# One decoder block on one core: other places in the input stage, quarter rows for the last block, and w_down's sums at every fourth product

## The chip, the cores and the metric

The kernel runs on one core of a Trainium2 chip. The metric is the device time of one execution in microseconds. A core has five engines that run their own instruction streams side by side: TensorE (PE, matmuls, with its weight loads as PEld), VectorE (DVE), ScalarE (ACT), GpSimd (POOL) and SyncE (SP), which here does nothing but issue transfers. Transfers can also be issued by ACT and POOL; all of them run on the same 16 DMA engines. An instruction waits for what it needs at its place in its engine's stream, and everything behind it on that engine waits too.

## The reference

One layer: RMSNorm, one wide input projection, two mixers side by side (a gated causal mixer over chunks of 128 positions, and a dilated window attention), a gated merge, an output projection with residual, then a gated MLP with a causal convolution, and a final RMSNorm. Sequence 1024, width 1024, MLP width 2816, everything in float32.

```python
h = rms_norm(x, mix_norm_g)
proj = h @ w_in                       # 1024 x 5888, split into z_a | q | k | v | gates
y_a = chunked_spatial_gating(gelu(z_a), gmlp_norm_g, w_spatial, b_spatial)
q, k = rope(q, positions), rope(k, positions)
y_b = dilated_mixture_attention(q, k, v)
merged = sigmoid(g_A) * (y_a @ w_branch_a) + sigmoid(g_B) * (y_b @ w_branch_b)
x = x + merged @ w_out
h2 = rms_norm(x, ffn_norm_g)
a, val = split(h2 @ w_up)
x = x + (gelu(causal_dwconv3(a)) * val) @ w_down
return rms_norm(x, final_norm_g)
```

## The kernel before

**Arithmetic.** Every float32 product is made of three fast ones: an operand is split into a high part, copied by ACT into the fast format ("hi"), and a low part, the difference, made by DVE or POOL ("lo"); hi·hi, hi·lo and lo·hi are added up in PSUM. On top of that the large products are done with a Strassen-like scheme of seven half-size products per pair of column blocks, named P1 to P7 and run in the order P1, P6, P2, P7, P5, P4, P3. In the input stage one such product is 12 matmuls of 128x512 (`in_product`, line 541). P2 is added into the PSUM bank of P1, P4 into that of P7, P3 into that of P5, so P4 can only begin when DVE has read P7's result out of its bank (line 576), and P3 only when it has read P5's (line 578). The bank's owner and its follower are two places apart, so DVE has the length of one product for that.

**Stages.** (1) `beginning`: the first two column blocks are computed plainly from the raw, not yet normalised x (tile `pl`, line 614), while x arrives in eight slices per half, `x_half(kt, h)`; the rows' root mean squares come from x in row layout (`square_row`, `root`), are put on a diagonal (`diagonal`, line 418), spread over the partitions by TensorE (`spread`, line 424), and multiplied into x (`scale_x`, line 484). `raw_left(h, kt)` makes hi (line 478, ACT) and lo (line 479, DVE) of the raw x; `left_of` makes those of the scaled x and of its sums (lines 448, 449, 454, 455). The first half is needed with the opposite sign, which its diagonal carries. A chain of small DVE steps for the rotary tables (`rot_tables`, run by `some(n)`) is strewn in between. (2) The remaining column blocks through `in_product`, with attention beside them. (3) From the last attention block on, DVE also makes sums of w_down's quarters for the last stage: `wd_load(kt)` loads four tiles of 256 KB (line 1057), `wd_sums(kt)` makes four sums of them (line 1068, 128x512 each) and stores them (tile `wT`, line 1070), for kt from 0 to 10, with two sets of buffers. (4) Branch products, w_out, the MLP's products (lines 1403 to 1932). (5) The down projection (tile `dn`, line 2195) into four blocks of rows for each half; its last product P3 is closed block by block, and a block is finished by an addition (line 2263), a sum of squares (line 2220), `finish_rms` (lines 2316 and 2321), and two halves of a row that are scaled and stored: the lower by ACT on ACT's queue (lines 2228, 2229), the upper by DVE on SP's queue (lines 2230, 2233).

**What sets the order.** TensorE's instructions stand in the order in which the code is written, over the whole kernel. Those of DVE and ACT do so in `beginning`, in the first 18 products after it, and at the end of the kernel; elsewhere a scheduler places them, and it places SP's transfers everywhere, by estimated costs.

## Time and profile before

| | us |
|---|---|
| median of 3 runs | 1364.97 |
| lowest and highest of them | 1363.93, 1366.61 |
| the profiled execution's own time | 1365.51 |
| its span from first to last instruction | 1363.6 |
| PE, DVE, ACT, POOL busy in the span | 1353.7, 1034.4, 645.0, 307.3 |

The span leaves out 1.9 us of the execution's time, and the profiled execution stands 0.54 us above the median. In a timeline a row gives the start, the time that the merged instructions take, the engine, the line, the operation, output and input tiles, the sizes, a count, and in brackets how long the engine had been idle and what ended that. Matmuls follow each other faster than one takes, so the start of one row to the start of the next is the measure, not the sum of durations.

### The profile page before, as it was taken

Reading aid. Unit: us, or ns where it says so; the run is one execution under the profiler, and the core shown is the slowest. Engines: PE = TensorE matmul, PEld = TensorE weight load, DVE = VectorE, ACT = ScalarE, POOL = GpSimd, SP = SyncE. Lnnn points to the kernel's source line nnn. Section 1 sums busy time; section 2 is a strip of 40 time slices with the busy share of each in tenths; the row PEclk is TensorE's granted clock in tenths of the full one; section 3 lists DMA queues with packets and bytes.
Section 4 is the critical chain, followed back from the end, with each engine's and each line's share of the span. In section 5 each row is a group of like instructions: output and inputs, shape, how many; then the busy total and the mean of one; then the engine's idle time right before and its main releaser. Section 6 shows DMA issues by size and latency. Waiting matters only on the chain.

```text
span 1363.6 us, 19146 instructions
## 1 busy us (share of the span) xinstructions
PE 1353.7 (99%) x6408; PEld 1126.2 (83%) x6408; DVE 1034.4 (76%) x1878; ACT 645.0 (47%) x1267; POOL 307.3 (23%) x301
## 2 busy tenths in 40 slices
PE   9999999999999999999999999999999999999997
PEld 8878888888888888888888888888888888888886
DVE  6988686767877987759789878676666668676674
ACT  7762555556543325435456344433343335354453
POOL 1123000001330000210011236666555653000002
PEclk9999999999999999999999999999999999999999
DMA  9535553544438994884751133333323327986663
GB/s 339 118 97 178 132 171 102 156 151 129 134 111 278 324 322 171 285 276 150 252 151 59 62 101 108 117 102 121 118 102 105 108 101 278 387 308 218 203 203 123
DMA packets 144577, 236.99 MB, mean 174 GB/s; under 512 B 13920, under 2 KB 57952, under 8 KB 144480
## 3 DMA queue, kind: packets, MB, share of 16 engines
q1 hardware_dynamic: 141952, 231.53, 51.5%
q0 software_dynamic: 1088, 2.10, 0.9%
q10 hardware_dynamic: 1440, 2.16, 0.4%
q8 instruction: 50, 0.82, 0.2%
q14 instruction: 47, 0.39, 0.1%
HBM read 167.77 MB, written 64.29 MB: 170 GB/s over the span
## 4 chain that ended last, share of the span: by engine, by line
PE 95%; DVE 1%; DMA 1%; ACT 1%; SPq 1%; issue 0%; POOL 0%; ACTq 0%; DVEq 0%; POOLq 0%
PE in_P L541 25%; PE uP L1932 21%; PE dn L2195 15%; PE up L1932 8%; PE wo_P L1764 6%; PE pa L1403 5%; PE pl L614 3%; PE pu L917 2%; PE pu L1912 2%; PE pb L1403 2%; PE pp L901 1%; PE sc L862 1%; PE sc L863 1%; SPq L757 1%; PE ht L1668 1%; PE pm L734 0%
## 5 line engine op out<-in xcount | busy, mean ns | idle before, releaser
L541 PE MATMUL in_P<-R,G 128*128 128x512 f32 x1008 | 243.9, 394 | 0.0
L541 PEld LDWEIGHTS in_P<-R,G 128*128 128x128 f32 x1008 | 185.5, 188 | 37.7 <-issue 0.3
L2195 PE MATMUL dn<-R 128*128 128x512 f32 x924 | 209.6, 389 | 0.0
L2195 PEld LDWEIGHTS dn<-R 128*128 128x128 f32 x924 | 173.4, 188 | 36.0
L170 ACT ACTIVATE R<-up 128x512 fp32r<-128x512 f32 x130 | 78.5, 626 | 119.3 <-DVE up L279 45.3
L312 ACT ACTIVATE G<-wr 128x512 fp32r<-128x512 f32 x126 | 78.9, 628 | 101.2 <-PE in_P L541 60.9
L541 PE MATMUL in_P<-G,G 128*128 128x512 f32 x504 | 123.5, 394 | 0.6 <-DVE C L576 0.3
L1932 PE MATMUL uP<-G,R 128*128 128x512 f32 x504 | 121.2, 389 | 0.0
L1932 PE MATMUL uP<-R 128*128 128x512 f32 x504 | 121.1, 389 | 0.0
L1932 PE MATMUL up<-G,R 128*128 128x512 f32 x504 | 120.5, 389 | 0.0
L1932 PEld LDWEIGHTS up<-G,R 128*128 128x128 f32 x504 | 94.6, 188 | 20.2
L1932 PEld LDWEIGHTS uP<-G,R 128*128 128x128 f32 x504 | 94.6, 188 | 19.8
L1932 PEld LDWEIGHTS uP<-R 128*128 128x128 f32 x504 | 94.6, 188 | 19.7
L541 PEld LDWEIGHTS in_P<-G,G 128*128 128x128 f32 x504 | 92.5, 188 | 20.6 <-issue 1.1
L313 DVE TENSOR_TENSOR G<-wr,G 128x512 fp32r<-128x512 f32 x126 | 88.2, 700 | 26.0 <-ACT G L312 24.8
L171 POOL TENSOR_TENSOR R<-up,R 128x512 fp32r<-128x512 f32 x55 | 82.7, 1506 | 58.8 <-ACT R L170 53.7
L171 DVE TENSOR_TENSOR R<-up,R 128x512 fp32r<-128x512 f32 x75 | 67.1, 898 | 18.4 <-ACT R L170 18.2
L170 ACT ACTIVATE R<-db 128x512 fp32r<-128x512 f32 x77 | 48.1, 626 | 57.6 <-PE dn L2195 46.6
L171 DVE TENSOR_TENSOR R<-db,R 128x512 fp32r<-128x512 f32 x77 | 53.6, 699 | 26.3 <-ACT R L170 26.1
L1403 PE MATMUL pa<-R,G 128*128 128x512 f32 x288 | 67.9, 389 | 0.0
L968 POOL TENSOR_TENSOR ld<-ld,w 128x256 f32<-128x256 f32 x16 | 11.3, 725 | 233.5 <-DVE w L956 233.5
L1403 PEld LDWEIGHTS pa<-R,G 128*128 128x128 f32 x288 | 54.0, 188 | 11.2
(286 smaller groups left out, 2438.4 us busy)
## 6 DMA issues: line engine op xcount, KB each, us to landing
up<-in_w_up_dram SPq DMA_DIRECT2D x44, 512.0 KB, 3.6
wr<-in_w_in_dram SPq DMA_DIRECT2D x42, 512.0 KB, 4.1
dA<-gd SPq DMA_DIRECT2D x55, 256.0 KB, 4.8
wd<-in_w_down_dram SPq DMA_DIRECT2D x44, 256.0 KB, 5.1
wT<-wd SPq DMA_DIRECT2D x44, 256.0 KB, 3.8
dS<-gS SPq DMA_DIRECT2D x44, 256.0 KB, 4.4
db<-wT SPq DMA_DIRECT2D x44, 256.0 KB, 4.4
gd<-Y SPq DMA_DIRECT2D x42, 256.0 KB, 2.0
```

The source lines that it names most:

```text
L170: nc.scalar.activation(hi, src, AF.Copy)
L171: fn = lambda: lo_eng.tensor_tensor(lo, src, f32(hi), ALU.subtract)
L312: lambda: nc.scalar.activation(op[:, 0], src, AF.Copy),
L313: lambda: nc.vector.tensor_tensor(op[:, 1], src, f32(op[:, 0]), ALU.subtract),
L541: nc.tensor.matmul(acc, op[:, w, kt, :], left[LEFT[name], kt][:, a, :], start=opened and i == 0, stop=i == len(HIGH_FIRST) - 1, skip_group ...
L614: nc.tensor.matmul(lead_banks[b][:, cs], raw_x[h, kt][:, a, c * P : (c + 1) * P], lead_op(kt, w, cs), start=kt == 0 and p == 0 and cs.star ...
L917: nc.tensor.matmul(pu[:, h * HD : (h + 1) * HD], self.pT[:, i, :], vt[:, h * HD : (h + 1) * HD], start=i % n == 0, stop=i % n == n - 1,)
L1403: nc.tensor.matmul(acc, unit[a][kt // 4][:, kt % 4, :], two(R, 8 * h + kt)[:, b, :], start=n == 0 and i == 0, stop=n == len(kts) - 1 and i ...
L1764: nc.tensor.matmul(acc, left[LEFT[name], kt][:, a, blk * P : (blk + 1) * P], out_ops[s][:, w, :], start=name not in SHARED and kt == 0 and ...
L1912: nc.tensor.matmul(acc, plain_up[which, k][:, w, kt, :], left[f"A{h + 1}{k + 1}", kt][:, a, :], start=n == 0 and i == 0, stop=n == KT - 1 ...
L1932: nc.tensor.matmul(acc, op[:, w, kt, :], left[LEFT[name], kt][:, a, :], start=opened and i == 0, stop=i == len(HIGH_FIRST) - 1, skip_group ...
L2195: nc.tensor.matmul(accs[blk], dops[s][:, 0, a, blk * P : (blk + 1) * P], dops[s][:, 1, w, :], start=SEQ[j] not in CONTINUES and kt == 0 an ...
```

## The change

The change has four groups of edits.

*Input stage.* The load of `positions` goes from ACT's queue (a step of the rotary chain) to SP's queue, ahead of x's fourth slice. The diagonals are made by ACT instead of DVE, both with a positive sign; the first half's minus goes into `ngain`, a copy of the norm's gains that POOL negates once, which `scale_x` then reads. Six rotary steps instead of three of them stand before the second wave of splits, so the chain runs three steps ahead from there. The spread of the first half stands after the first four matmuls of kt 6 instead of before them. The low part of the second half's first slices is written after the squares, and the second pair of slices before the rotary steps. In the first product's place, ACT reads out P1's bank before it makes P6's high part.

*w_down's sums.* They are taken up at every fourth product, counted from the product before the stage, instead of at each P1 and P5.

*Residual.* Two blocks are loaded by one transfer.

*Last block.* `last_blocks` takes the place of the last call: the block before it is scaled and stored first, its lower half on SP's queue; the last block's upper half is added, squared, scaled and stored in two quarters, with one more addend in `finish_rms`.

```diff
+    pos = lent[:, 11 * NB * (ROT // 2) :][:, 0:NB].bitcast(I32)
     for kt in range(1, KT):
+        if kt == 3:
+            nc.sync.dma_start(pos, positions)
         if kt == 6:
             load_rows(0, range(4))
...
-            nc.vector.tensor_scalar(dg, ident, rs, (-1.0, 1.0)[h], ALU.mult, ALU.mult)
+            nc.scalar.activation(dg, ident, AF.Copy, scale=rs)
...
+    ngain = lent[:, 6 * P - KT : 6 * P]
     def scale_x(h, kt, bc):
-        xs = x_half(kt, h)
-        nc.vector.scalar_tensor_tensor(xs, xs, chan[:, kt : kt + 1], bc, ALU.mult, ALU.mult)
+        xs, gain = x_half(kt, h), (ngain, chan)[h]
+        nc.vector.scalar_tensor_tensor(xs, xs, gain[:, kt : kt + 1], bc, ALU.mult, ALU.mult)
...
         both(lead_parts(5))
-        some(6)
+        some(9)
...
+        nc.gpsimd.tensor_scalar(ngain, chan[:, 0:KT], -1.0, None, ALU.mult)
         root(0)
-        both(raw_left(0, 6, 1))
+        both(raw_left(0, 6, 1), lead_parts(6))
         diagonal(0)
-        both(lead_parts(6))
         both(raw_left(0, 7, 1), lead_parts(7))
-        bc0 = spread(0)
-        lead_step(first, 6)
-        both(raw_left(1, 0))
+        for p in range(3):
+            if p == 1:
+                bc0 = spread(0)
+            for b in first:
+                lead_pass(b, 6, p)
+        h1_hi, h1_lo = raw_left(1, 0)
+        h1_hi()
...
         root(1)
+        h1_lo()
         for kt in range(KT):
             scale_x(0, kt, bc0)
+        both(raw_left(1, 2))
+        some(3)
         diagonal(1)
-        some(3)
-        both(raw_left(1, 2), raw_left(1, 4), raw_left(1, 6))
+        both(raw_left(1, 4), raw_left(1, 6))
...
-        p6[0]()
         x_sum(2, 1)
         in_product(FIRST, "P1")
+        p6[0]()
         p6[1]()
...
-        if wd is not None and name in ("P1", "P5"):
-            wd_sums(wd_step - 1)
-            wd_load(wd_step)
+        if wd is not None:
+            if wd_step % 4 == 0:
+                wd_sums(wd_step // 4 - 1)
+                wd_load(wd_step // 4)
             wd_step += 1
...
+    def store_lower(b, rs, queue):
+        nc.scalar.activation(Y[:, b, lower], Y[:, b, lower], AF.Copy, scale=rs)
+        queue.dma_start(out_t[:, b, lower], Y[:, b, lower])
+    def store_upper(b, rs, cs):
+        nc.vector.scalar_tensor_tensor(
+            Y[:, b, cs], Y[:, b, cs], rs, final_bc[:, cs], ALU.mult, ALU.mult
+        )
+        nc.sync.dma_start(out_t[:, b, cs], Y[:, b, cs])
+    def last_blocks(acc):
+        b = 3
+        ahead = finish_rms(nc, small, mhalf, sqs[b - 1], f"f_{b - 1}", nc.vector)
+        store_lower(b - 1, ahead, nc.sync)
+        quarter = [slice(HALF + i * 256, HALF + (i + 1) * 256) for i in range(2)]
+        for i, cs in enumerate(quarter):
+            nc.vector.tensor_tensor(
+                Y[:, b, cs], Y[:, b, cs], acc[:, i * 256 : (i + 1) * 256], ALU.add
+            )
+            jk = dp.tile([P, HALF], F32, name=f"fj_{b}_{1 + i}", tag="fj")
+            nc.scalar.activation(
+                jk[:, 0:256], Y[:, b, cs], AF.Square, accum_out=sqs[b][:, 1 + i : 2 + i]
+            )
+        store_upper(b - 1, ahead, quarter[0])
+        rs = finish_rms(nc, small, mhalf, sqs[b], f"f_{b}", nc.gpsimd, nc.vector)
+        store_upper(b - 1, ahead, quarter[1])
+        store_lower(b, rs, nc.scalar)
+        for cs in quarter:
+            store_upper(b, rs, cs)
```

Three places in the instruction streams follow; line numbers of the changed kernel are its own.

ACT in the input stage, second half of x, before the change: `C` with `ms_x` are the squares of rows, `pl` the plain product's result, `G<-X` and `R<-X` the high parts of x.

```order
L400 ACTIVATE C_105,ms_x_368<-C_105 128x1024
L631 ACTIVATE C_103<-pl_188,rs_x_320 128x512
L478 ACTIVATE G_76<-X 128x2x512
L478 ACTIVATE G_77<-X 128x2x512 x2
L448 ACTIVATE R<-X 128x2x512 x2
L631 ACTIVATE C_103<-pl_190,rs_x_320 128x512
```

The same place on ACT with the change:

```order
L403 ACTIVATE C_105,ms_x_371<-C_105 128x1024
L636 ACTIVATE C_103<-pl_189,rs_x_324 128x512
L481 ACTIVATE G_76<-X 128x2x512
L421 ACTIVATE YC<-ident,rs_x_379 128x128 x4
L481 ACTIVATE G_77<-X 128x2x512 x2
L451 ACTIVATE R<-X 128x2x512 x2
L636 ACTIVATE C_103<-pl_191,rs_x_324 128x512
```

Four instructions that write the second diagonal (`YC<-ident`) now stand on ACT between the first pair of high parts and the next two; another four stand ahead of x's last slice of the first half.

SP's transfers at the start of the w_down stage, before: `wd_0` and `wd_1` are the loads for kt 0 and 1, `wT` the stores of the sums.

```order
L666 DMA gated<-C_103 128x512
L1057 DMA wd_0_4280<-in_w_down_dram 128x512
L1057 DMA wd_0_4282<-in_w_down_dram 128x512
L1057 DMA wd_0_4284<-in_w_down_dram 128x512
L1057 DMA wd_0_4286<-in_w_down_dram 128x512
L1057 DMA wd_1_4363<-in_w_down_dram 128x512
L1057 DMA wd_1_4365<-in_w_down_dram 128x512
L1057 DMA wd_1_4367<-in_w_down_dram 128x512
L1057 DMA wd_1_4369<-in_w_down_dram 128x512
L1070 DMA wT_157<-wd_0_4286 128x512
L1070 DMA wT_155<-wd_0_4282 128x512
```

The same with the change:

```order
L1062 DMA wd_0_4267<-in_w_down_dram 128x512
L671 DMA gated<-C_103 128x512
L1328 DMA ya<-mixd 128x1024 x2
L1075 DMA wT_158<-wd_0_4267 128x512
L1075 DMA wT_156<-wd_0_4263 128x512
L1075 DMA wT_157<-wd_0_4261 128x512
L1075 DMA wT_159<-wd_0_4265 128x512
L1062 DMA wd_1_4346<-in_w_down_dram 128x512
L1062 DMA wd_1_4348<-in_w_down_dram 128x512
L1062 DMA wd_1_4350<-in_w_down_dram 128x512
L1062 DMA wd_1_4352<-in_w_down_dram 128x512
```

The loads for kt 0 now stand ahead of the last `gated` store and of two loads of `ya`, and those for kt 1 behind the four stores of the sums of kt 0, which wait for DVE.

ACT at the end of the kernel, before: `fj` is a square of a half row of a block, `Y<-Y,fr_f` the scaling of its lower half.

```order
L2220 ACTIVATE fj_1_11626,fsq_10661<-Y 128x512
L2228 ACTIVATE Y<-Y,fr_f_11611 128x512
L2229 DMA out_dram<-Y 128x512
L2220 ACTIVATE fj_1_11650,fsq_10666<-Y 128x512
L2228 ACTIVATE Y<-Y,fr_f_11635 128x512
L2229 DMA out_dram<-Y 128x512
L2228 ACTIVATE Y<-Y,fr_f_11659 128x512
L2229 DMA out_dram<-Y 128x512
```

And with the change:

```order
L2232 ACTIVATE fj_1_11623,fsq_10658<-Y 128x512
L2246 ACTIVATE Y<-Y,fr_f_11608 128x512
L2247 DMA out_dram<-Y 128x512
L2246 ACTIVATE Y<-Y,fr_f_11644 128x512
L2267 ACTIVATE fj_1_11649,fsq_10663<-Y 128x256
L2267 ACTIVATE fj_2_11652,fsq_10663<-Y 128x256
L2246 ACTIVATE Y<-Y,fr_f_11660 128x512
L2247 DMA out_dram<-Y 128x512
```

The scaling of the third block (`fr_f_11635`, now `fr_f_11644`) has moved ahead of the last block's squares, which are two of half the width, and its store has left ACT's stream.

39 lines of the change are left out of this document (18 added, 21 removed).

## The prediction

> **What bounds the kernel now.** I read the page's first part, then the chain that ended last, then TensorE's own timeline where it isn't gapless, and last the rows of the other engines there.
>
> ```profile
> PE 1353.7 (99%) x6408; PEld 1126.2 (83%) x6408; DVE 1034.4 (76%) x1878; ACT 645.0 (47%) x1267; POOL 307.3 (23%) x301
> ...
> 1147.06 209.45 PE dn L2195 x924
> ```
>
> TensorE is busy for 99% of the span, and no matmul is added or taken away. In the down projection 924 matmuls take 209.45 us without a wait, 0.2267 us each; that is my measure of a matmul of 512 columns. What the change can move is therefore only TensorE's waits beside it and the tail after its last matmul. These are the two stages that the change touches, TensorE alone:
>
> ```profile
> 62.93 5.39 PE L541 MATMUL in_P<-G,G 128*128 128x512 f32 x22
> 68.56 0.73 PE L541 MATMUL in_P<-G,G 128*128 128x512 f32 x2 [0.23 <-DVE G L455]
> 69.13 1.08 PE L541 MATMUL in_P<-R,G 128*128 128x512 f32 x4
> ...
> 446.88 2.88 PE L541 MATMUL in_P<-G,G 128*128 128x512 f32 x12
> 450.09 2.97 PE L541 MATMUL in_P<-G,G 128*128 128x512 f32 x12 [0.32 <-DVE C L576]
> 453.09 3.00 PE L541 MATMUL in_P<-G 128*128 128x512 f32 x12
> 455.93 11.04 PE L541 MATMUL in_P<-R,G 128*128 128x512 f32 x48
> ...
> 485.85 5.88 PE L541 MATMUL in_P<-G,G 128*128 128x512 f32 x24
> 491.56 0.62 PE L541 MATMUL in_P<-G 128*128 128x512 f32 x2
> ```
>
> From 62.93 to 69.13 stand 24 matmuls, 5.44 us by the measure in 6.20: 0.76 lost, at the end to a low part of line 455. From 446.88 to 455.93 stand 36, 8.16 us in 9.05: 0.89 lost, since P4 waits until DVE has read P7's bank (line 576), and P3 likewise. From 485.85 to 491.56 stand 24, 5.44 in 5.71: 0.27 lost. So the input stage can give at most 0.76 us and w_down's sums 1.16.
>
> **Input stage.** First the edits of positions and chain.
>
> ```profile
> 7.09 0.36 ACTq L2350 DMA_DIRECT2D ones<-in_positions_dram  x1
> 20.77 0.69 DVE L479 TENSOR_TENSOR R<-X,R 128x512 fp32r<-128x512 f32 x1 [1.54 <-ACT R L478]
> ...
> 22.07 0.63 ACT L478 ACTIVATE R<-X 128x512 fp32r<-128x512 f32 x1 [0.72 <-DMA X<-in_xt_dram]
> 24.02 1.06 ACT L478 ACTIVATE G<-X 128x1024 fp32r<-128x1024 f32 x1 [0.58 <-DMA X<-in_xt_dram]
> 26.25 5.35 DVE L484 SCALAR_TENSOR_TENSOR X<-X,chan,rs_bc 128x512 f32<-128x512 f32 x8
> 31.09 2.00 ACT L478 ACTIVATE G<-X 128x1024 fp32r<-128x1024 f32 x2
> 31.52 0.87 DVE L418 TENSOR_SCALAR YC<-ident,rs_x 128x128 f32<-128x128 f32 x4
> 33.03 3.49 DVE L479 TENSOR_TENSOR G<-X,G 128x1024 fp32r<-128x1024 f32 x3
> 33.45 1.06 PE L424 MATMUL rs_bc<-YC,ones 128*128 128x128 f32 x8
> 36.44 2.71 DVE L484 SCALAR_TENSOR_TENSOR X<-X,chan,rs_bc 128x512 f32<-128x512 f32 x4
> ...
> L2388 ACT ACTIVATE YC<-ones 128x128 f32<-128x128 f32 x16 | 3.5, 296 | 0.0
> L599 ACT ACTIVATE G<-wr_lead,chan 128x256 fp32r<-128x256 f32 x2 | 1.0, 508 | 2.3 <-DMA wr_lead<-in_w_lead_dram 1.5 <-DMA chan<-in_per_channel_dram 0.8
> ```
>
> The positions' transfer costs one issue, 0.36 us, now on SP ahead of x's fourth slice. ACT waits for x's later slices at 22.07 and 24.02 whatever SP's issue does, since the same bytes stand ahead of them; I take 0, and not more than 0.36, which the work between kt 3 and kt 7 covers.
>
> The diagonals leave DVE (0.87 us for four) and come to ACT. No row shows ACT making one. Its nearest rows: 128x128 with a constant scale, 16 in 3.5 us, 0.22 each in sequence; 128x256 with a scale per partition, 0.508 us, which at half the width (ACT's 1024 columns take 1.06 and 512 take 0.63, so 0.11 less) is 0.40. I take 0.30, between them, so 1.2 us for four. The first four fall before 24.02, where ACT had waited 0.72 and 0.58 us for x: nothing. The second four stand behind the first high part of the row at 31.09, which ends at 32.1: they run to 33.3, in time for the spread at 33.45, and the next two high parts end at 34.3 and 35.3 instead of 33.1 and 34.3. DVE ends `scale_x` at 31.6, waits for 32.1, makes a low part (1.22) to 33.35, three rotary steps (0.73) to 34.1, then waits for 34.3 and makes two more low parts: 36.75. Before, it was at 36.44. So DVE gains the 0.87 us and loses it again to ACT: +0.3 us, which passes through DVE's gapless chain to the wait at 68.56. With 0.22 each it is 0, with 0.40 each +0.75. Below, 0.76 could go if DVE were ahead after all.
>
> ```profile
> 53.33 0.63 ACT L312 ACTIVATE G<-wr 128x512 fp32r<-128x512 f32 x1 [3.92 <-DVE wr L279]
> ```
>
> Reading P1's bank before making P6's high part gains nothing: that high part waits for DVE's line 279 until 53.33 anyway, and what stands behind it on ACT waits for `x_sum(2, 1)`, which DVE makes after that line, at the same place as before. Moving the first half's spread behind four matmuls, the negation on POOL and the late `h1_lo` (DVE's stream keeps its order there) are 0: work of the same size on engines that aren't waited for at that time. The three rotary steps that run earlier (0.73) fall into DVE's wait of 1.54 us ahead of 20.77. Sum of the stage: +0.3, from -0.76 to +0.75.
>
> **w_down's sums.**
>
> ```profile
> 440.82 5.91 DMA wd<-in_w_down_dram
> ...
> 442.49 0.69 DVE L1068 TENSOR_TENSOR wd<-wd,wd 128x512 f32<-128x512 f32 x1 [0.93 <-DMA wd<-in_w_down_dram]
> 446.85 0.69 DVE L1068 TENSOR_TENSOR wd<-wd,wd 128x512 f32<-128x512 f32 x1 [1.14 <-DMA wd<-in_w_down_dram]
> 449.26 0.68 DVE L576 TENSOR_TENSOR C<-C,in_P 128x512 f32<-128x512 f32 x1
> ...
> 484.04 2.74 DVE L1068 TENSOR_TENSOR wd<-wd,wd 128x512 f32<-128x512 f32 x4
> ```
>
> DVE lost 0.93 and 1.14 us waiting for loads of w_down just ahead of the reading at 449.26 that TensorE waits for. At 484.04 four sums in a row, 2.74 us, stand shortly ahead of the reading that costs 0.27. With the change the stream of DVE holds the sums of kt 2 and 3 at the same places; those of kt 6 to 10 are pulled apart, with two or three between readings where four stood. The 0.27 then goes. At kt 2 and 3 the loads come sooner by the megabyte of kt 0, fetched ahead of the stage, and later because those of kt 1 stand behind four stores. I take it that the 1.14 goes; the splitting that follows still waits for ACT, so I count half of the 0.89: -0.45. Together -0.7.
>
> The bounds: all waits go, -1.16. Or the loads of kt 1, now behind four stores and perhaps as long under way as the chain's load (5.91 us), are waited for as those of kt 2 and 3 were, and nothing goes: 0.89 once for kt 1 and once more for what it passes on, +1.8.
>
> The residual's merged loads save SP four issues in a stage where TensorE shows no wait: 0, whatever they cost, as long as operands lead by whole steps.
>
> **Last block.**
>
> ```profile
> 1356.54 0.69 DVE L2263 TENSOR_TENSOR Y<-Y,dn 128x512 f32<-128x512 f32 x1 [1.03 <-PE dn L2195]
> 1357.80 0.18 ACT L2220 ACTIVATION_READ_ACCUMULATOR fj<-Y 128x1 f32 x1
> 1357.89 0.71 ACT L2228 ACTIVATE Y<-Y,fr_f 128x512 f32<-128x512 f32 x1
> 1358.31 0.55 POOL L2321 TENSOR_TENSOR fr_f<-fm_f,mhalf 128x1 f32<-128x1 f32 x1 [2.17 <-DVE fm_f L2316]
> 1359.01 0.72 ACT L2228 ACTIVATE Y<-Y,fr_f 128x512 f32<-128x512 f32 x1 [0.41 <-POOL fr_f L2321]
> 1359.77 0.34 ACTq L2229 DMA_DIRECT2D out_dram<-Y  x1
> ...
> DMA to landing us min/median/max: 2.0/2.1/2.8
> ...
> L965 DVE TENSOR_TENSOR st<-pu,w 128x256 f32<-128x256 f32 x8 | 3.4, 422 | 0.2
> L696 ACT ACTIVATE junk_v<-V 128x256 bf16<-128x256 f32 x8 | 3.2, 404 | 0.0
> L600 DVE SCALAR_TENSOR_TENSOR G<-wr_lead,chan,G 128x256 fp32r<-128x256 f32 x2 | 1.0, 484 | 4.3 <-ACT G L599 4.3
> scr<-st SPq DMA_DIRECT2D x16, 132.0 KB, 2.4
> ```
>
> TensorE ends at about 1356.5, so 7.1 us of the span are tail. ACT's stream shows why it is long: after the square it scales the third block (0.71), issues its store (0.34), and only then, at 1359.01, scales the last block, whose store leaves at 1359.77. With the change the third block is done before. The addition in quarters is 0.42 each (the row of 128x256 out of PSUM), the squares 0.40: the second addition ends at about 1357.35, its square's sum is there at 1357.87 instead of 1357.98, the root at 1358.75 instead of 1358.86. ACT scales from 1358.8 and issues at 1359.55, 0.22 earlier. DVE's two quarters, 0.48 each, end at 1359.75, and the last store, half as large, leaves at 1359.78. I take -0.25. Stores of 256 KB landed after 2.0 to 2.8 us; one of 132 KB (`scr`) takes 2.4 in the median. If the last quarter needs 2.0, the gain is 0.5; if the extra addend on POOL (bounded by the 0.55 us of POOL's row) and 2.8 us for the landing come on top, the loss is 0.6.
>
> **Sum.** +0.3 - 0.7 - 0.25 = -0.65 us. The profiled execution took 1365.51, so 1364.86 by it; it stood 0.54 above the median, and from the median of 1364.97 it is 1364.3. The ends add up to -2.4 (-0.76, -1.16, -0.5) and +3.15 (+0.75, +1.8, +0.6): 1362.6 and 1368.1. A measurement of this kernel tells about 0.2%, 2.7 us, from no change: its three runs lie that far apart.
>
> **Rivals.**
> *All waits go, 1362.6.* DVE has 0.87 us less twice over in the input stage, and less crowding in the w_down stage; if ACT's diagonals cost 0.22 and the loads land ahead of DVE, all of 1.92 us and half a microsecond of the tail go. Against it stands ACT's gapless row of high parts at 31.09.
> *The stores block the loads, 1368.6: slower.* SP issues in order, so the loads of the next kt wait until DVE has made the last sum of the one before. The reading of P7's bank (0.68) must begin within 2.04 us of P7's end, as P5 lasts 2.72; at 449.26 it came 2.38 after 446.88. It decides once loads push the readings of further kt over that point; at 0.89 each, as there, four of them cost 3.6: 1365.0 + 0.3 - 0.25 + 3.6. For it speaks the wait of 1.14 us that loads already cause; against it that the loads for kt 2 to 10 stood behind stores before as well.
> *ACT becomes the bound, 1365.5.* Diagonals at 0.40 and nothing gained from the sums: +0.75 - 0.25.
> *The quarters don't overlap, 1366.1.* If the second quarter's transfer only begins when the first has landed, the end is 1359.3 plus twice 2.4, 1364.1, where 1359.77 + 2.8 is 1362.6: 1.5 later, and +0.3 - 0.7 + 1.5 in all. Against it: all sixteen stores of the end, from two queues, landed within 2.8 us of their issue. The Trainium skill, page "DMA: Bandwidth & Descriptors", section "Measured (HBM→SBUF, 128 partitions, SWDGE, issued from GpSimd)", advises against such splits: transfers should be batched to a megabyte, as small ones are dominated by descriptors; between its figures for 64 KB and 1 MB (0.95 and 6.15 us) I estimate 1.3 us for 128 KB and 2.0 for 256, so two quarters would take 0.6 us more than one half, and the tail by it +0.35 in place of -0.25. Its table is for loads from another queue; no run here shows a quarter's store yet.
>
> **Chances.** The forecast 0.50; all waits gone 0.20; the stores block the loads 0.10; ACT the bound 0.15; no overlap 0.05. Faster by over 0.2% means under 1362.2: half of the second case, as three runs scatter around 1362.6, and 0.02 of the first, 0.12. Slower means over 1367.7: the third case, 0.10. Within: 0.78. The range from 1362.6 to 1366.4 leaves out the third case and the lower part of the second; the forecast's own is 1363.4 to 1365.6.
>
> **What would show it.** In the changed kernel's timeline: four ACT rows of 128x128 near 21 and near 32, of 0.3 us in sequence; DVE's second `scale_x` between 36.4 and 36.8; TensorE's 24 matmuls before 69 still with some 0.8 to 1.1 us over; no wait of TensorE near 488, and under 0.5 near 450; ACT's last scaling at about 1358.8 on the old clock, and 0.1 to 0.4 us less from the last matmul to the end. I am wrong if TensorE shows new waits between 418 and 545, or if its products after 69 stand earlier by over half a microsecond.

## The result and the profile after

The changed kernel takes 1368.6 us (median of 21 runs, 1366.0 to 1371.6), the kernel before 1365.98 in the same number of runs (1363.7 to 1367.7). The ratio is 1.0021, with a 95% interval from 1.0015 to 1.0027: 2.0 to 3.7 us slower, where 0.65 us less was forecast. Two runs among those of the experiments, one of `input_only` (2282 us) and one of the kernel before (4860 us), are left out of the ratios. The profiled execution of the changed kernel took 1369.46 us, with a span of 1367.7, 4.1 more than before.

TensorE alone, in the same stretches of the changed kernel's timeline that the prediction showed of before, with two more places where it now waits:

```profile
61.73 1.98 PE L546 MATMUL in_P<-G,G 128*128 128x512 f32 x8
63.90 0.73 PE L546 MATMUL in_P<-G,G 128*128 128x512 f32 x2 [0.19 <-DVE G L458]
65.03 3.22 PE L546 MATMUL in_P<-G,G 128*128 128x512 f32 x12 [0.40 <-DVE G L458]
68.50 0.73 PE L546 MATMUL in_P<-G,G 128*128 128x512 f32 x2 [0.25 <-DVE G L458]
69.08 2.89 PE L546 MATMUL in_P<-R,G 128*128 128x512 f32 x12
...
99.01 0.91 PE L739 MATMUL pm<-wspT,C 128*128 128x128 f32 x6 [0.93 <-DVE C L742]
...
448.08 3.00 PE L546 MATMUL in_P<-G,G 128*128 128x512 f32 x12
453.01 2.97 PE L546 MATMUL in_P<-G,G 128*128 128x512 f32 x12 [1.93 <-DVE C L581]
...
488.75 5.60 PE L546 MATMUL in_P<-G,G 128*128 128x512 f32 x24
494.19 2.88 PE L546 MATMUL in_P<-G 128*128 128x512 f32 x12
...
507.79 5.60 PE L546 MATMUL in_P<-G,G 128*128 128x512 f32 x24
514.88 2.32 PE L546 MATMUL in_P<-G 128*128 128x512 f32 x9 [1.49 <-DVE C L583]
```

The same two further places in the kernel before:

```profile
97.98 0.91 PE L734 MATMUL pm<-wspT,C 128*128 128x128 f32 x6 [0.52 <-DVE C L737]
...
505.16 5.60 PE L541 MATMUL in_P<-G,G 128*128 128x512 f32 x24
510.60 2.88 PE L541 MATMUL in_P<-G 128*128 128x512 f32 x12
```

Subtracting starts of the same matmuls tells where the time went. At 69 us the two kernels stand level (69.08 against 69.13). At 99 the changed one is 1.03 behind. At the P5 that starts as P7 ends, in the w_down stage, it is 1.20 behind (448.08, 446.88), at the P4 after it 2.92 (453.01, 450.09): 1.7 lost at one reading of P7's bank. At P3 near 494 it is 2.63 behind (494.19, 491.56), so 0.3 was regained, the 0.27 at 488 among it. At P3 near 515 it is 4.28 behind (514.88, 510.60): 1.65 lost again. From there to the last matmul 0.1 more is lost, and the tail behind it is 0.4 shorter. So w_down's stage lost 3.1 us, and the places ahead of 99 us 1.0.

SP's queue at the start of the w_down stage, first of the changed kernel, then of the one before:

```profile
419.30 0.85 SPq L1328 DMA_DIRECT2D ya<-mixd  x2
421.92 4.05 SPq L1075 DMA_DIRECT2D wT<-wd  x4
426.02 1.89 SPq L1062 DMA_DIRECT2D wd<-in_w_down_dram  x4
...
433.55 2.12 SPq L1075 DMA_DIRECT2D wT<-wd  x2
435.72 0.42 SPq L1062 DMA_DIRECT2D wd<-in_w_down_dram  x1
437.75 1.92 SPq L1075 DMA_DIRECT2D wT<-wd  x2
439.71 3.52 SPq L1062 DMA_DIRECT2D wd<-in_w_down_dram  x7
```

```profile
418.25 4.04 SPq L1057 DMA_DIRECT2D wd<-in_w_down_dram  x8
426.06 2.50 SPq L1070 DMA_DIRECT2D wT<-wd  x4
...
435.22 0.42 SPq L1057 DMA_DIRECT2D wd<-in_w_down_dram  x1
436.65 0.32 SPq L1070 DMA_DIRECT2D wT<-wd  x1
437.02 4.21 SPq L1057 DMA_DIRECT2D wd<-in_w_down_dram  x7
```

The loads of kt 1 used to leave by 422.3, with those of kt 0; now they leave from 426.02, behind four stores that wait for DVE's sums. What follows on DVE in the changed kernel:

```profile
432.83 0.69 DVE L1073 TENSOR_TENSOR wd<-wd,wd 128x512 f32<-128x512 f32 x1 [1.72 <-DMA wd<-in_w_down_dram]
...
446.64 0.69 DVE L1073 TENSOR_TENSOR wd<-wd,wd 128x512 f32<-128x512 f32 x1 [3.38 <-DMA wd<-in_w_down_dram]
...
452.19 0.68 DVE L581 TENSOR_TENSOR C<-C,in_P 128x512 f32<-128x512 f32 x1
...
512.71 1.42 DVE L1073 TENSOR_TENSOR wd<-wd,wd 128x512 f32<-128x512 f32 x2 [2.64 <-DMA wd<-in_w_down_dram]
514.05 0.68 DVE L583 TENSOR_TENSOR C<-C,in_P 128x512 f32<-128x512 f32 x1
```

The sums of kt 1 wait 1.72 us, so their stores and the loads of kt 2 behind them are later, and the first sum of kt 2 waits 3.38 us (the 0.93 of before). From it DVE works without a gap to the reading of P7's bank at 452.19, for which TensorE waits. At 512.71 two sums of kt 9, whose loads are still under way, stand straight ahead of the reading of P5's bank.

### The profile page after: what moved, and what is told of

It is laid out like the page before. It is cut to its first block, busy times and chain, and to the rows that moved or that the text cites. A ratio compares the mean times of both kernels' runs of the same rounds, so it can differ in the third digit from the quotient of the medians.

```text
span 1367.7 us, 19150 instructions
## 1 busy us (share of the span) xinstructions
PE 1353.6 (99%) x6408; PEld 1124.8 (82%) x6408; DVE 1031.9 (75%) x1873; ACT 647.5 (47%) x1277; POOL 305.2 (22%) x303
## 4 chain that ended last, share of the span: by engine, by line
PE 92%; DVE 3%; DMA 2%; ACT 1%; issue 1%; POOL 0%; SPq 0%; POOLq 0%; DVEq 0%; ACTq 0%
PE in_P L546 23%; PE uP L1943 21%; PE dn L2206 15%; PE up L1943 8%; PE wo_P L1775 6%; PE pa L1414 5%; PE pl L619 3%; PE pu L922 2%; PE pu L1923 2%; PE pb L1414 2%; PE pp L906 1%; DMA wd<-in_w_down_dram 1%; PE sc L867 1%; PE sc L868 1%; DMA ya<-mixd 1%
## 5 line engine op out<-in xcount | busy, mean ns | idle before, releaser
L546 PE MATMUL in_P<-G 128*128 128x512 f32 x252 | 62.1, 393 | 1.9 <-DVE C L583 1.9
```

Of the source, the lines that this page charges most:

```text
L546: nc.tensor.matmul(acc, op[:, w, kt, :], left[LEFT[name], kt][:, a, :], start=opened and i == 0, stop=i == len(HIGH_FIRST) - 1, skip_group ...
```

## The experiments

Each label is a kernel. Ratios are to the kernel before, in runs of the same session; a thousandth is 1.37 us.

**One group of edits at a time.** The change was cut into its groups. `wd_only` makes the following edit in the kernel before, and `wd_undone` takes it back out of the changed kernel; `input_only` is the kernel before with the input stage's edits, `end_only` with those of the last block and the residual.

```diff
-        if wd is not None and name in ("P1", "P5"):
-            wd_sums(wd_step - 1)
-            wd_load(wd_step)
+        if wd is not None:
+            if wd_step % 4 == 0:
+                wd_sums(wd_step // 4 - 1)
+                wd_load(wd_step // 4)
             wd_step += 1
```

> The kernel before with the change's third group alone, w_down's sums at every fourth product. Theory A, from the two traces: the loads of kt 1 now stand behind the four stores of the sums of kt 0, the delay is passed on, and DVE waits for loads just ahead of readings of banks that TensorE waits for. By the changed kernel's trace that is 1.6 us more at 450 and 1.5 us anew at 513, and 0.2 regained at 488: 2.9 us over the kernel before, with both waits in its trace. Rival B, the loss of the whole change (2.6 us between the medians) comes from the input stage and the waits here are made up elsewhere: within 0.8 us of the kernel before.

> The changed kernel with w_down's sums back at each P1 and P5; the input stage and the last block stay changed. Theory A: the waits at 450 and 513 are gone or as before, and the time is that of the kernel before or up to 0.5 us less by the tail, unless the input stage's loss of 1.0 us near 85 to 98 belongs to the edits: then 0.7 us more. Rival B: as slow as the changed kernel, 2.6 us over the kernel before.

> The kernel before with the edits of the input stage alone. In the changed kernel's trace TensorE starts 0.3 us sooner and is 1.2 us ahead at 24 us, all of which is given back at three waits for DVE before 69 us; then it loses 1.0 us between 85 and 99, because the load of the spatial weights leaves SP's queue 1.2 us later, behind a transfer of the bias whose issue took 2.9 us instead of 1.7. Theory C: that loss comes with the edits, +1.0 us. Rival D: that issue's length differs from run to run in any kernel, and the edits are worth nothing: within 0.4 us of the kernel before, with an issue near 1.7 us or one that differs without its time.

> The kernel before with the last block in quarters and the residual's merged loads alone. From the changed kernel's trace, from the last block's addition to the end of the span 6.76 us instead of 7.06: theory E, the last two quarters land sooner, -0.3 us. Rival F: the scaling of the last block starts no sooner than before (2.52 us after the addition, 2.47 before), so nothing is gained and the 0.3 us is the scatter of the landing: within 0.1 us of the kernel before, with a tail that differs from 6.76.

| kernel | us, median | ratio (95%) |
|---|---|---|
| wd_only | 1369.76 | 1.0026 (1.0016 to 1.0036) |
| wd_undone | 1365.55 | 0.9995 (0.9987 to 1.0004) |
| input_only | 1364.39 | 0.9989 (0.9980 to 0.9998) |
| end_only | 1366.54 | 1.0004 (0.9996 to 1.0013) |

Theory A holds: w_down's sums alone cost 3.6 us, and taking them out of the change takes as much away (1.0021 less 0.9995). TensorE's two waits, for the readings of P7's and P5's banks, stand in the timeline of `wd_only`:

```profile
451.60 4.58 PE L541 MATMUL in_P<-G,G 128*128 128x512 f32 x12 [1.85 <-DVE C L576]
...
515.57 4.22 PE L541 MATMUL in_P<-G 128*128 128x512 f32 x12 [2.24 <-DVE C L578]
```

These rows show a second price of a wait. The 12 matmuls behind the first wait took 4.58 us, where they took 2.97 in the changed kernel's profile: the granted clock of TensorE is 0.50 from 452.2 to 455.6 us, and again from 517.0 to 520.4. `k1early_2` below has such a stretch behind its wait of 2.28 us; the profiles of the changed kernel, `last`, `k1early` and `wd_only_2` have none, with waits of 1.93, 1.94, 2.05 and 2.30, so what decides it stays open. It bears on the medians: six of the twelve runs of `wd_only` have a mean granted clock of 0.997 or less and took 1371.4 us in the mean, the other six 1368.2; of the changed kernel's 21 it is eight, 1369.8 against 1368.3. None of the 90 runs of the kernel before in the experiments' sessions that enter the ratios is under 0.998.

The time of `input_only` is 0.3 to 2.7 us less than before, so theory C falls: the 1.0 us between 85 and 99 doesn't belong to the input stage's edits. It comes from the issue of a bias transfer, `b_bc`, of which twelve stand ahead of the load of the spatial weights. The twelve, before and after, and the scaling on DVE that waits for POOL and those weights, after:

```profile
73.31 8.67 SPq L757 DMA_DIRECT2D b_bc<-in_b_spatial_dram  x12
```

```profile
73.25 9.92 SPq L762 DMA_DIRECT2D b_bc<-in_b_spatial_dram  x12
```

```profile
89.14 0.48 DVE L710 TENSOR_SCALAR C<-C,rs_v 128x512 f32<-128x512 f32 x1 [2.07 <-POOL rs_v L706]
```

The fourth of the twelve takes 1.67 us before and 2.93 after. In every one of the eighteen profiles one of them is long: the fourth in `wd_undone` (1.67), the fifth in `wd_only` (2.13), the sixth in `input_only` and `end_only` (1.54, 1.58). 2.93 stands in the changed kernel's profile alone; the ten others with the same input stage have 1.5 to 1.8. So the first half of rival D holds. Its second half, that these edits are worth nothing, is not settled: the time says otherwise, but the product behind the wait near 68 starts at 68.84 us in the median of the seven profiles with the old input stage and at 68.87 in that of the eleven with the new one. `end_only` decides neither for theory E nor for rival F by its time, which is within the scatter; its tail is taken up below.

**What makes the two waits.** Two repairs, each of one suspected cause, and two other orders of loads and stores, all in the changed kernel. The load of kt 1 alone:

```diff
                 wd_sums(wd_step // 4 - 1)
-                wd_load(wd_step // 4)
+                if wd_step != 4:
+                    wd_load(wd_step // 4)
+            if wd_step == 1:
+                wd_load(1)
             wd_step += 1
```

> The changed kernel with one load moved: that of kt 1, at the product after the first one of the stage instead of four later. It now stands on SP's queue ahead of the four stores of the sums of kt 0, as in the kernel before; from kt 2 on SP's and DVE's streams are those of the changed kernel. Theory A1, the wait at 450 grew because the loads of kt 1 stood behind those stores and passed their delay on to the loads of kt 2 and 3: the wait of 1.9 us falls to 0.3 to 0.6, the one at 513 stays, 1.4 us less than the changed kernel. Rival A2, it grew because DVE's row of sums ahead of the reading is too long, whatever the loads do: the same time as the changed kernel.

The last steps alone:

```diff
-            if wd_step % 4 == 0:
-                wd_sums(wd_step // 4 - 1)
-                wd_load(wd_step // 4)
+            at = (0, 4, 8, 12, 16, 20, 24, 28, 32, 33, 36, 40)
+            if wd_step in at:
+                wd_sums(at.index(wd_step) - 1)
+                wd_load(at.index(wd_step))
             wd_step += 1
```

> The changed kernel with the sums of kt 8 and 9 and their successors' loads back at the products where the kernel before has them (33rd and 36th, instead of 36th and 40th); all ahead of that is as in the changed kernel. Theory A1: the wait at 513 is gone, since the sums of kt 9 no longer stand ahead of the reading of P5's bank while their loads are under way; the one at 450 stays at 1.9 us; 1.5 us less than the changed kernel. Rival A3, the wait at 513 is what the wait at 450 passes on: both stay, and the time is that of the changed kernel.

Loads written ahead of sums:

```diff
             if wd_step % 4 == 0:
+                wd_load(wd_step // 4)
                 wd_sums(wd_step // 4 - 1)
-                wd_load(wd_step // 4)
             wd_step += 1
```

> The changed kernel with the load of the next kt written ahead of the sums of the one before, at the same products. On SP's queue every four loads now stand ahead of the four stores that were made ahead of them, for all kt and not in pairs of eight. Theory A1: loads land before DVE comes to the sums, both waits go or fall under 0.5 us each, 2.5 to 3.2 us less than the changed kernel. Rival A2: DVE has the same 44 sums to make in the same products, so the waits stay, and the time is within 0.8 us of the changed kernel's.

Loads a whole step sooner:

```diff
                 wd_sums(wd_step // 4 - 1)
-                wd_load(wd_step // 4)
+                for kt in range(2) if wd_step == 0 else (wd_step // 4 + 1,):
+                    wd_load(kt)
             wd_step += 1
```

> The changed kernel with two kt loaded at the start of the stage and each further one four products sooner. The buffers of the next kt but one are then free only when the stores have read them, so those loads wait on SP's queue for the stores' landing. Theory A1: the wait at 450 goes (1.6 us), later ones depend on the wait for buffers: between 3.2 and 1.0 us less than the changed kernel. Rival A2: the same time as the changed kernel.

| kernel | us, median | ratio (95%) |
|---|---|---|
| k1early | 1368.27 | 1.0014 (1.0003 to 1.0024) |
| last | 1366.89 | 1.0006 (0.9996 to 1.0015) |
| loadfirst | 1364.37 | 0.9988 (0.9980 to 0.9997) |
| ahead | 1374.5 | 1.0059 (1.0045 to 1.0073) |

Each repair takes away its own wait and leaves the other. `k1early`, TensorE: 24 matmuls without a gap from 446.45, and a wait at 512.96 (one of 0.84 at 469.57 is new; in a second execution it is missing):

```profile
446.45 5.63 PE L546 MATMUL in_P<-G,G 128*128 128x512 f32 x24
...
512.96 2.98 PE L546 MATMUL in_P<-G 128*128 128x512 f32 x12 [2.05 <-DVE C L583]
```

`last`, TensorE, the other way round (506.35 to 511.96 is 5.61, 0.17 over 24 matmuls):

```profile
446.61 3.00 PE L546 MATMUL in_P<-G,G 128*128 128x512 f32 x12
451.54 2.96 PE L546 MATMUL in_P<-G,G 128*128 128x512 f32 x12 [1.94 <-DVE C L581]
...
506.35 5.78 PE L546 MATMUL in_P<-G,G 128*128 128x512 f32 x24
511.96 2.88 PE L546 MATMUL in_P<-G 128*128 128x512 f32 x12
```

So the two waits come and go apart, and rivals A2 and A3 fall by the profiles. The gains (1.0 and 2.0 us by the ratios, 1.4 and 1.5 forecast) agree within their intervals; by its time alone `k1early` can't be told from the changed kernel. `loadfirst` keeps the places of the change and only writes loads ahead of sums: 4.5 us less than the changed kernel by the ratios (0.0033), more than the 2.5 to 3.2 forecast. It trades both waits for two of 0.9 elsewhere. `ahead` went wrong for theory A1: SP's loads waited 34.8 us in 30 cases for stores to land, so that their buffers were free, against 2.0 us in 2 cases in the changed kernel, and TensorE waited 1.25 us near 452 and 4.9 near 499. A load that is written sooner than its buffer is free blocks the queue like a store that is early. How much of that does harm is a matter of degree: `loadfirst`, among the fastest, has 19.2 us of such waits in 15 cases.

**Both repairs, the smallest cause, and the queue.** Both repairs at once, in the changed kernel:

```diff
-            if wd_step % 4 == 0:
-                wd_sums(wd_step // 4 - 1)
-                wd_load(wd_step // 4)
+            at = (0, 4, 8, 12, 16, 20, 24, 28, 32, 33, 36, 40)
+            if wd_step in at:
+                wd_sums(at.index(wd_step) - 1)
+                if wd_step != 4:
+                    wd_load(at.index(wd_step))
+            if wd_step == 1:
+                wd_load(1)
             wd_step += 1
```

> The changed kernel with both repairs at once: the load of kt 1 one product into the stage, and the sums of kt 8 and 9 at the products of the kernel before. Theory A1, the two waits have two separate causes, both named: no TensorE wait over 0.6 us near 450 and near 513, and the time within 0.6 us of the kernel with w_down's sums undone (0.45 us under the kernel before). Rival A4, the waits only move, as the 0.8 us near 469 in the run with kt 1 alone repaired might show: new waits of 0.8 us or more elsewhere in the stage, and 1 us or more over the kernel before.

One load moved, in the kernel before:

```diff
-        if wd is not None and name in ("P1", "P5"):
-            wd_sums(wd_step - 1)
-            wd_load(wd_step)
+        if wd is not None:
+            at = (0, 5, 8, 12, 15, 19, 22, 26, 29, 33, 36, 40)
+            if wd_step in at:
+                wd_sums(at.index(wd_step) - 1)
+                wd_load(at.index(wd_step))
             wd_step += 1
```

> The kernel before with a single load moved: that of kt 0, at the first product of the stage's start, one sooner; every sum and every other load is written at the old product. Its stores then stand on SP's queue ahead of the loads of kt 1, the pairing of the changed kernel. Theory A1: that alone makes the wait near 450, 1.9 us in place of 0.3, and the kernel is 1.2 to 1.6 us slower than before; no wait at 513. Rival A2, the spacing of four products makes it: within 0.4 us of the kernel before.

The stores on another queue, in the changed kernel:

```diff
-            nc.sync.dma_start(wsum[n][kt], t)
+            nc.gpsimd.dma_start(wsum[n][kt], t)
```

> The changed kernel with the stores of w_down's sums issued by POOL, so that no load stands behind a store on SP's queue; sums and loads are written at the products of the changed kernel. Theory A1, what delays the loads is SP's order: loads of kt 1 leave by 421, and the waits near 450 and 513 fall under 0.5 us each: 2.5 to 3.2 us less than the changed kernel. Rival A5, the loads wait for their buffers (two sets) whatever queue the stores stand on: the waits stay, and the time is within 0.8 us of the changed kernel's, or over it where the stores land later from POOL's queue.

Loads ahead of sums at the old places, in the changed kernel:

```diff
-            if wd_step % 4 == 0:
-                wd_sums(wd_step // 4 - 1)
-                wd_load(wd_step // 4)
+            at = (1, 5, 8, 12, 15, 19, 22, 26, 29, 33, 36, 40)
+            if wd_step in at:
+                wd_load(at.index(wd_step))
+                wd_sums(at.index(wd_step) - 1)
             wd_step += 1
```

> The changed kernel with loads written ahead of sums as in the run that did so, but at the products of the kernel before (every three and a half). Theory A1: what counts is that each kt's loads leave ahead of the stores of the one before: as fast as that run, 1.5 to 2.5 us under the kernel before. Rival A6, the sparser places are worth something by themselves once the loads are in time: 0.8 us or more slower than that run.

| kernel | us, median | ratio (95%) |
|---|---|---|
| both | 1364.79 | 0.9987 (0.9978 to 0.9996) |
| k0early | 1366.09 | 1.0002 (0.9992 to 1.0012) |
| stpool | 1376.99 | 1.0074 (1.0062 to 1.0087) |
| lf35 | 1364.82 | 0.9986 (0.9977 to 0.9995) |

With `both` the time is 1.1 us under that of `wd_undone` (0.9987, 0.9995), where theory A1 had 0.6 at most; the intervals overlap, and rival A4 falls by the time. Its profile does show a wait of 1.26 at 508.5, where theory A1 had none over 0.6, so waits of that size come and go in this stage. `k0early` contradicts A1 as it was put: SP's and DVE's streams up to kt 6 are those of `wd_only`, the loads of kt 1 behind the stores of kt 0, and there was no wait near 450 and no loss, as rival A2 has it. In `stpool` the loads of kt 1 left from 418.1 to 420.5 and the waits at 450 and 513 are gone, as theory A1 has it. The time went the way of rival A5: stores from POOL's queue landed after 6.0 us in the median (3.6 from SP's in the changed kernel), the loads waited for the buffers, and TensorE waited elsewhere, 2.35 us at 459 and 3.62 at 498. SP's own waits there, total, times, longest:

```profile
SPq L1062 <- DMA wT<-wd: 55.3, 25, 6.5
```

`lf35` is as fast as `loadfirst`; A6 falls. TensorE's waits in its profile, all of them, with none in the w_down stage:

```profile
PE warm L395 <- POOL ident masks.py:199: 1.7, 1, 1.7
PE pm L739 <- DVE C L742: 0.3, 1, 0.3
PE in_P L546 <- DVE G L458: 0.2, 1, 0.2
```

`loadfirst`, `lf35`, `both` and `input_only` are 1.5 to 2 us faster than the kernel before, and can't be told apart; so how much of it is the sums and how much the input stage stays open.

**Slack and landing.** Four further executions, of kernels that had run, were to tell chance from a cause in `k0early`'s place.

> Another execution of the kernel before with kt 0's load one product sooner. Theory A7, slack and landing: the fourth load of kt 2 is issued about 7.5 us ahead of P7's first matmul (as in the first execution, 439.4 against 446.7) and lands 4 to 5.7 us later; DVE reads P7's bank 5.6 us after the landing; TensorE waits 1 to 1.7 us near 450 where the landing takes over 5 us, and under 0.4 us where it takes 4. Rival A8, the spacing of four products is what makes the wait: under 0.4 us in every execution of this kernel.

> The same once more: theory A7 has the wait near 450 in some of these executions and in some not, always by the landing of kt 2's fourth load; rival A8 has it in none.

> Another execution of the kernel before with w_down's sums at every fourth product. Theory A7: the wait near 450 is 1.5 to 2 us where kt 2's fourth load takes over 5 us to land, and shrinks one for one with an earlier landing. Rival A8: 1.9 us again, whatever that load takes. The wait near 513, whose sums stand ahead of the reading of P5's bank, by either: 1.4 to 2.3 us.

> Another execution of the changed kernel with kt 1's load repaired. Theory A7: its kt 2 loads leave 2 us sooner, so no wait over 0.4 us near 450 even where a load takes 5.7 us to land; the wait near 513 stays at 1.4 to 2.3 us. Rival A8: 1.5 us or more near 450, since the spacing is that of the changed kernel.

They took 1365.08, 1365.47, 1369.30 and 1367.73 us, the kernel before 1364.37 beside them. One rule fits the profiles in which DVE comes to the sums of kt 2 in one row: from the first of them, which starts when the load that it needs has landed, DVE has 5.6 us of work up to the reading of P7's bank, and that reading must begin within 2.04 us of P7's end. So the sum must start 3.5 us ahead of P7's end, and TensorE waits for what is missing. (The expectations say P7's first matmul, but the time that they mean is P7's end, at which P5 starts: 447.06 in the first execution of `k0early`.) "None" stands for no idle time in the timeline; the 24 matmuls of P5 and P4 still took up to 0.45 us over their 5.44 there.

| execution | first sum of kt 2 | P7's end | lead | TensorE's wait |
|---|---|---|---|---|
| changed | 446.64 | 448.08 | 1.44 | 1.93 |
| last | 445.17 | 446.61 | 1.44 | 1.94 |
| wd_only | 445.23 | 446.87 | 1.64 | 1.85 |
| wd_only_2 | 444.04 | 446.44 | 2.40 | 1.10 |
| wd_undone | 444.51 | 447.24 | 2.73 | 0.76 |
| k0early | 443.57 | 447.06 | 3.49 | none |
| k0early_3 | 443.73 | 447.27 | 3.54 | none |
| end_only | 445.37 | 449.01 | 3.64 | none |
| k1early | 442.74 | 446.45 | 3.71 | none |
| k0early_2 | 442.33 | 446.15 | 3.82 | none |
| k1early_2 | 441.36 | 445.94 | 4.58 | none |
| both | 441.39 | 446.23 | 4.84 | none |

The kernel before and `input_only` are not in the table, since a later load held up a later sum there (by 1.14 and 0.24 us; by 0.31 in `both`): before, the first sum has a lead of 4.39 and TensorE waited 0.32 all the same. `loadfirst`, `lf35`, `ahead` and `stpool` have another order.

So A8 holds in its letter (no wait in three executions of `k0early`) and fails in `k1early`, which has the spacing of four and no wait here in two; `wd_undone`, with the old places, has a small one. What acts is the lead, as A7 has it. It has two parts. The order gives the time of issue: kt 2's last three loads leave in a row that starts 9.9 us ahead of P7's end in the kernel before (437.02), 10.8 in `k1early`, 8.6 in `k0early` and 8.4 in the changed kernel (439.71). The load that decides, the last of the three, is issued 7.0 to 7.3 us ahead of P7's end in the four executions that waited longest, 7.7 to 7.9 in the three of `k0early` and 8.2 to 9.6 in the others. The landing is the other part: that load lands 3.6 to 5.7 us after its issue, in kernels with the old places too (before 3.7, `input_only` 3.6, `end_only` 5.4, `wd_undone` 5.5). The order of the changed kernel spends the slack, and then a long landing shows one for one: 5.5 us there, 5.3 in `wd_only`, 4.1 in `k0early`. Part of the lateness is an issue on SP's queue just ahead of that load, in `wd_only` and in `k0early`:

```profile
438.24 1.08 SPq L1057 DMA_DIRECT2D wd<-in_w_down_dram  x1
```

```profile
438.42 0.43 SPq L1057 DMA_DIRECT2D wd<-in_w_down_dram  x1
```

In `wd_only` a transfer of 16 KB on an instruction queue begins at 438.1, in `k0early` at 437.0, while SP is waiting for a store anyway. In the changed kernel it falls on the store just ahead of the row (0.71 us for 0.32); in the kernel before it falls on a load (1.18 us), where there is slack for it. Whether the three short landings of `k0early` (4.0 to 4.1 us, against 4.8 to 5.7 in the four executions that waited longest) are chance, stays open: the streams of the two kernels agree up to kt 6.

## Why the prediction was wrong, step by step

**w_down's sums: the step that failed.** The term was -0.7, with bounds of -1.16 and +1.8; it measured +3.6 by the ratio of `wd_only`, and the stage lost 3.1 in the changed kernel's profile, which shows no loss of clock there. The prediction's own sign of being wrong, new waits between 418 and 545, is in the timeline. Three things in its working failed. "Together -0.7" took it that the wait of 1.14 goes because kt 0's loads come sooner; that wait did go and those loads do come sooner, but kt 1's leave 6 us later, which the text had and didn't follow to kt 2, where the wait of 0.93 became 3.38. The bound of +1.8 priced a late load at twice the 0.89 of before; the loss at one reading alone was 1.7, since a lead that is short costs one for one. And for kt 6 to 10 the step counted how many sums stand between readings, not whether their loads have landed: two sums of kt 9 ahead of the reading of P5's bank cost 1.65. The sub-step on 488 was right: its 0.27 went.

The rival that the stores block the loads named the right place and the right limit (the reading must begin within 2.04 us of P7's end), and its 1368.6 is the measured median, by luck. Its mechanism was right at one place of the two; it had four waits of 0.89 where there were one of 1.93 and one of 1.49. "The loads for kt 2 to 10 stood behind stores before as well", which spoke against it, was true and beside the point, as the slack for them was spent by kt 1.

**Input stage: sizes right, sign not settled.** A diagonal on ACT was taken as 0.30; four take 1.26, 0.31 each. ACT, then DVE, of the changed kernel:

```profile
31.49 1.26 ACT L421 ACTIVATE YC<-ident,rs_x 128x128 f32<-128x128 f32 x4
```

```profile
36.02 2.71 DVE L489 SCALAR_TENSOR_TENSOR X<-X,chan,rs_bc 128x512 f32<-128x512 f32 x4
```

From DVE's first low part of the last slice to the second `scale_x` it was 11.33 us (25.11 to 36.44) and is 11.48 (24.54 to 36.02): +0.15, where +0.3 was counted. But the group alone gives -1.5 us (0.9980 to 0.9998), which leaves +0.3 outside, while the profiles stand level at 69 us (medians 68.84 and 68.87, above). What starts the chain, the landing of x's last slice, came at other times: DVE's first `scale_x` begins at 26.25 before, 25.69 with the change, 26.24 in `wd_undone` and 25.45 in `input_only`. One profile each doesn't show whether that is the edits' doing, so where the gain comes from is not settled. The 24 matmuls before 69 now take 7.35 us for 5.44, 1.91 over, against 0.8 to 1.1 that were forecast: TensorE came 1.2 us sooner and waited for the same DVE.

**Last block: size right, reason wrong.** The term was -0.25. From the start of the last matmul to the end of the span it is 7.5 us in all seven profiles with the old end and 7.1 to 7.3 in ten with the new one (7.6 in `stpool`): -0.4. ACT's last scaling was to start 0.2 sooner. It starts 2.94 after the last matmul's start (1363.46), before 2.89: POOL's root starts 2.19 after it in both, with an addend more ahead of it, and takes 0.71 for 0.55. POOL and ACT at the end of the changed kernel:

```profile
1362.71 0.71 POOL L2363 TENSOR_TENSOR fr_f<-fm_f,mhalf 128x1 f32<-128x1 f32 x1 [0.36 <-DVE fm_f L2358]
```

```profile
1363.46 0.72 ACT L2246 ACTIVATE Y<-Y,fr_f 128x512 f32<-128x512 f32 x1 [1.15 <-POOL fr_f L2363]
```

Nor is the gain a sooner landing: the last store lands 6.25 us after the last matmul's start in both kernels. Before, it is ACT's half, issued at 1359.77 and landed 2.6 us later; with the change it is the last quarter, issued at 1364.40 and landed 2.4 us later. What differs is behind that, 1.27 us to the end of the span before and 0.90 with the change. SP ends the program with seven waits for landings, 0.06 us apart. Before, the first of them is the one for the last landing, and six more follow it; with the change the first four are done by 1365.1, and the last landing ends the seventh. SP's waits there (total, times, longest), before and with the change:

```profile
SPq L2459 <- DMA out_dram<-Y: 2.4, 1, 2.4
```

```profile
SPq L2499 <- DMA out_dram<-Y: 1.6, 2, 1.3
```

So the size of this term came out by luck. The quarters overlap (the second is issued at 1364.40, the first lands at 1365.7), so that rival falls. From the figures of the Trainium skill, page "DMA: Bandwidth & Descriptors", section "Measured (HBM→SBUF, 128 partitions, SWDGE, issued from GpSimd)", the prediction estimated that two quarters take 0.6 us more than one half, and a tail longer by 0.35. The tail is shorter by 0.4, for the reason given; of the quarters themselves the trace is near that estimate, as the second landed 0.55 us later after the last matmul than the half did before (6.25, 5.70; its issue came 0.3 later as well).

**Residual: 0.** No run took it apart from the last block. TensorE shows no wait in the down projection in any of these profiles.

**The sum and the scatter.** The runs have the groups at about +3.6, -1.5 and +0.5, each give or take 1.3, against +2.9 for the whole. The sum of the forecast went wrong by one term; the input stage's, off by 1.8 the other way by its ratio, made up for part of it.

## What to carry to other kernels

Before a load or a store is moved on a queue that issues in order, follow what stands behind it for more than one round of its buffers, and write down the lead of each load over the work that another engine waits for: a lead that is just long enough costs nothing in one execution and its full lateness in the next. Where two buffers are in turn, loads belong ahead of the stores of the round before, not further ahead than their buffer is free. In counting what an engine has to do ahead of a critical reading, ask of each piece first whether its data are there.

## What the runs showed of the hardware that wasn't expected

*Issues beside a transfer on an instruction queue.* An issue of `b_bc` on SP takes 0.56 to 0.61 us, yet the fourth took 1.67 and 2.93 us in the profiles before and after, where a 16 KB transfer on an instruction queue began at 75.2 and 75.3 and took 1.30 and 2.38 us. In all eighteen profiles a transfer of this kind begins within 0.6 us of the start of the long issue, and the issue ends 0.37 to 0.39 us after the transfer. That SP waits for it is argued from these times; no row shows it. In the changed kernel's profile 1.0 us more of TensorE's time hung on it than before, through one load and POOL.

*Half the clock behind a wait.* In `wd_only`, `k1early_2`, `ahead` and `stpool` the granted clock is 0.50 for 3.4 us or more, behind or within a wait of TensorE of 1.85 to 4.9 us; elsewhere between the first 8 us and the last matmul no profile has such a stretch, and waits of 1.9 to 2.3 us in four other profiles brought none.

*TensorE's first microseconds.* In executions of one kernel, `k0early`, TensorE had 11 matmuls, of 256 columns but for the first, under way in each of the microseconds from 5 to 7 us, or 7. The two answers (busy time and count, granted clock, DMA's share and GB/s):

```profile
5.00:6.00 1.00, 1.00 (x11) 1.00 0.97 336
```

```profile
5.00:6.00 1.00, 1.00 (x7) 1.00 1.07 265
```

The granted clock reads 1.00 in both, but the trace has no record of it there: its first one, of the full clock, begins at 4.82 us in the first execution and at 7.19 in the second, and there the matmuls go over from starts 0.21 us apart to 0.12. At 7.6 us the quicker start is ahead by 1.1 us, which the waits for ACT near 8.8 and for DVE near 68 take back. The Trainium skill, page "TensorE: Matmul & The Clock Gate", section "Part 1: The HAM clock gate (the "warmup" mystery)", says that the array runs at half rate for its first 3.4 us or so, and that this varies between runs. By the spacing the trace agrees, with 3.2 and 5.5 us from TensorE's first matmul at 1.65.

*Stores from POOL's queue* landed after 6.0 us in the median, where those of the same size from SP's queue took 3.6.
